# RWKV chunk products: which half of the partitions a chunk's rows stand on, from fp and bvp to zp

## The chip, the cores and the metric

The kernel runs on one core of a Trainium2 chip. The metric is the device time of one execution in microseconds (us), with everything loaded from and stored to the chip's memory; smaller is better. TensorE (PE) does the matmuls out of SBUF into PSUM, VectorE (DVE) and ScalarE (ACT) read PSUM, GpSimd (POOL) works on SBUF alone, and SyncE (SP) issues nearly all DMA transfers. Each engine works through its instructions strictly in the order of the built program and waits at an instruction whose inputs or whose buffer are not ready.

## The reference, cut to what matters

One decoder layer on a 2048 x 1024 input: an input projection feeds two mixers, stick-breaking attention (8 heads of 64) and RWKV-7 time mixing (8 heads of 64). Their outputs are gated, joined, projected and normalised. The part that matters here is the RWKV recurrence, which the kernel computes in chunks of 64 tokens:

```python
def step(state, inp):
    r_t, w_t, k_t, v_t, kk_t, b_t = inp
    sa = jnp.einsum('bhij,bhj->bhi', state, -kk_t)
    state = (state * w_t[:, :, None, :]
             + sa[..., None] * b_t[:, :, None, :]
             + v_t[..., None] * k_t[:, :, None, :])
    y_t = jnp.einsum('bhij,bhj->bhi', state, r_t)
    return state, y_t
_, y = lax.scan(step, state0, (tm(r), tm(decay), tm(k), tm(v), tm(kk), tm(kk * a)))
```

## The kernel before

The program has two parts. The attention part fills the first 1060 us of the profile and is not touched. The RWKV part follows: 16 blocks (4 pairs of heads x 4 stretches of 512 tokens), and from the 15th block on the output projection beside them, which then runs alone to the end.

A block holds 8 chunks of 64 tokens for 2 heads, so 16 independent pairs of chunk and head. Chunks are written c = 2i + e, with e the parity, and h is the head. Each step of a block is a **burst** of 16 small matmuls (fp32, contraction over 64 rows, 64 output rows), which the profile counts as 32 since it records each in two passes. A matmul of this size needs one quadrant of the 128 x 128 array: the half of the partitions on which its inputs stand gives the rows, the half on which its output stands gives the columns. `HS[0]` and `HS[1]` are the two halves.

The steps of one block, in the order of its own data, with the names under which the trace shows them (buffer numbers are left out, so `x1` is `x`, `t16` is `t`, `n2` is `n`, `y0` is `y`):

- `stage_p` projects three inputs k, r and v (`pss`, lines 356 to 358), each 24 matmuls of 128x512 in fp16. These 72 `pss` matmuls of a block are what PE does between the small steps. Lines 385 to 389 read a finished projection (a copy on ACT, then two copies and a multiply-add on DVE). `pn` (L910) and `n` (L924) normalise the keys; POOL makes `bk` and `ar` from them.
- `stage_x`: `x` (L960), two bursts, gives the chunk matrices `mn` and `mt` (DVE, L965). `mn` goes to memory and comes back as 16 x 16 blocks (L972, L974), DVE inverts these in small steps (`invert`, L775 to L802), and the inverses go to memory (`dt`, L978) and come back as the tile `t` (L983) on the halves that the matmuls want.
- `stage_t`: transposes, and `bvp` (L1019) into `ab`.
- `stage_l`: `fp` (L1033) from `t` and `mn`, masked by DVE into `ft` (L1037); then `xp` (L1042) and twice `xp` (L1052), each followed by DVE additions into `rf`.
- `stage_z`: `zp` (L1066) into two PSUM banks from `rf` and `ab`, copied by ACT into `at` (L1070) and `zg` (L1074); then `mr`, `np` and `y`.
- `stage_c`: the chain over the chunks, 8 `sp` matmuls with a DVE step after each, and `yr` (L1130).

In `bvp`, `fp` and `zp` the parity e alone decides the half: for `fp` and `zp` chunk e's inputs and outputs both stand on `HS[e]`, so the 16 matmuls use two of the four quadrants in turn, and `bvp` uses the other two. `x`, `mr` and `yr` already use all four: there parity and head give rows and columns.

Three blocks are worked on at once. While block n runs its chain, block n+1 is in stages t, l and z, and block n+2 in `stage_p` and `stage_x`. The stages are Python generators, merged by `_side`: each `yield` says how long the piece of work is taken to be, and the generator that is least far on goes next. This gives the order in which the program is written. A scheduler of the framework then orders each engine's instructions by it and by readiness; a `burst()` keeps its matmuls together and is pulled forward. PSUM has 8 banks here: ring `mm` of 3 (projections and other single results), ring `z` of 2 (`z_ps`), ring `tr` of 2, and one more. A new tile of a ring waits until the oldest bank's readers are done.

Of the kernel before, what the change touches and what calls it, by code (L numbers as in the profile page):

```python
# [12 lines left out]
AF = mybir.ActivationFunctionType  # L13
ALU = mybir.AluOpType
# [4 lines left out]
P = 128  # L19
# [6 lines left out]
def _bc(ap, shape):  # L26
    return ap.to_broadcast(shape)
# [61 lines left out]
def trunk(nc, a, out):  # L89
# [3 lines left out]
    PE, V, A, G, DMA = nc.tensor, nc.vector, nc.scalar, nc.gpsimd, nc.sync  # L93
# [27 lines left out]
    def z_ps(name="z"):  # L121
        return pp.tile([P, TB], F32, tag="z", bufs=NM[1], name=name)
# [821 lines left out]
    def stage_x(n):  # L944
# [5 lines left out]
        mn = B["mn"] = []  # L950
# [26 lines left out]
        for m in range(2):  # L977
            DMA.dma_start(out=bass.AP(tensor=dt.tensor, offset=dt.offset + m * 66560,  # L978
                                      ap=[[1040, 64], [64, 16], [1, 16]]), in_=view(pr, 256 * m, [16, 16], [1, 16]))
        t16 = B["t16"] = rw.tile([P, 2, 8, 64], F32, tag="t16", name="t16")  # L980
        for e in range(2):
            for m in range(2):
                DMA.dma_start(out=t16[HS[e], m], in_=dt[m, e].rearrange("c s t -> s c t")[0:64])  # L983

# [3 lines left out]
    def stage_t(n):  # L988
# [21 lines left out]
        for i in range(4):  # L1010
            PE.transpose(ap[:, i * P:(i + 1) * P], ar[:, 0, 2 * i:2 * i + 2].rearrange("p c t -> p (c t)"), ident)
        yield 0.44
        A.activation(out=ab[:, :, :, 0, :].rearrange("p i h d -> p (i h) d"),
                     in_=ap.rearrange("p (c d) -> p c d", c=8), func=AF.Copy)
        bvp = z_ps("bvp").rearrange("p (c d) -> p c d", c=8)
        with burst():
            for i, h in IH:
                for e in (1, 0):
                    PE.matmul(bvp[HS[e], 2 * i + h], mn[i // 2][HS[1 - e], e, i % 2, h], zg[HS[1 - e], e, i, h],  # L1019
                              start=True, stop=True)  # L1020
        yield 0.9
        A.activation(out=ab[:, :, :, 1, :].rearrange("p i h d -> p (i h) d"), in_=bvp, func=AF.Copy)

    def stage_l(n):
# [3 lines left out]
        rf = B["rf"] = rw.tile([P, 8, 64], F32, tag="rf", name="rf")  # L1028
        fp = z_ps("fp").rearrange("p (c d) -> p c d", c=8)
        with burst():  # L1030
            for i, h in IH:
                for e in (1, 0):
                    PE.matmul(fp[HS[e], 2 * i + h], mn[i // 2][HS[e], e, i % 2, h], t16[HS[e], 0, 2 * i + h],  # L1033
                              start=True, stop=True)
        yield 0.9
        ft = rw.tile([P, 8, 64], F32, tag="ft", name="ft")
        V.tensor_tensor(out=ft, in0=fp, in1=_bc(fmask, [P, 8, 64]), op=ALU.mult)  # L1037
        xp = z_ps("xp").rearrange("p (c d) -> p c d", c=8)
# [18 lines left out]
    def stage_z(n):  # L1057
# [3 lines left out]
        at = rw.tile([P, 4, 2, 64], F32, tag="at", name="at")  # L1061
        zp = [z_ps("zp").rearrange("p (c m d) -> p c m d", c=4, m=2) for _ in range(2)]
        with burst():
            for i, h in IH:
                for e in (1, 0):
                    PE.matmul(zp[i // 2][HS[e], 2 * (i % 2) + h].rearrange("p m d -> p (m d)"), rf[HS[e], 2 * i + h],  # L1066
                              ab[HS[e], i, h].rearrange("p m d -> p (m d)"), start=True, stop=True)
        yield 1.8
        for g in range(2):
            A.activation(out=at[:, 2 * g:2 * g + 2].rearrange("p i h d -> p (i h) d"), in_=zp[g][:, :, 0, :],  # L1070
                         func=AF.Copy)
        for g in range(2):
            for e in range(2):
                A.activation(out=zg[HS[e], e, 2 * g:2 * g + 2].rearrange("p i h d -> p (i h) d"),  # L1074
                             in_=zp[g][HS[e], :, 1, :], func=AF.Copy)
        rq = B["rq"] = rw.tile([P, 8, 64], F32, tag="rq", name="rq")
# [245 lines left out]
```

## Time and profile before

| what | value |
|---|---|
| median of 3 runs | 1924.12 us (1922.18 to 1925.9) |
| the profiled execution, time | 1919.86 us |
| the profiled execution, span from first to last instruction | 1918.1 us |
| mean granted clock of TensorE | 0.971 |
| PE busy over the span | 1699.1 us (89%) |
| DVE busy | 1380.4 us (72%) |
| ACT busy | 859.7 us (45%) |
| POOL busy | 774.4 us (40%) |
| RWKV part: 16 blocks, about 41 us each | 1062 to 1746 us |
| output projection alone | 1746 to 1918 us |

Busy shares count overlapping matmuls once, so a PE that is busy all the time may still have slow instructions in it. An engine's idle time matters only where another engine waits for it in turn. The time of an execution is its span plus 1.8 us.

### The profile page before, as it was taken

The page shows a single profiled execution, that of the slowest core. Times are in us where ns is not written, and L with a number is a line of the kernel's source. Part 1 is how long each engine was busy: PE and PEld are TensorE (multiplying, and loading weights), DVE is VectorE, ACT ScalarE, POOL GpSimd, SP SyncE. Part 2 cuts the span into 40 slices and gives each one's busy share as a digit, 9 for nine tenths or more (in the row PEclk, how much of TensorE's full clock was granted, in tenths as well). Part 3 has the DMA queues.
Part 4 walks back from the last instruction along what each step waited for, and adds up shares of the span by engine and source line. Part 5 has one row for each costly group of instructions (what it writes and reads, how often), then busy time and mean ns, then how long its engine had stood idle before and what let it go on. Part 6 is the DMA issues. An engine that isn't in the chain of part 4 may idle for free. (4 is left out here: it accounts for less than half of the span.)

```text
span 1918.1 us, 38809 instructions
## 1 busy us (share of the span) xinstructions
PE 1699.1 (89%) x14816; PEld 1164.2 (61%) x14816; DVE 1380.4 (72%) x2871; ACT 859.7 (45%) x1706; POOL 774.4 (40%) x1114
## 2 busy tenths in 40 slices
PE   1879978999899998999997888898899998989998
PEld 1546655666565665667654455665565655667886
DVE  8967697678785778768766557878777777765543
ACT  0556576456564666546644333333332333422221
POOL 3615465356553556445444123233233322223322
PEclk9989999999999999999989989999999999999999
DMA  8341201222122221132111523322332333335442
GB/s 296 112 144 45 70 25 45 64 75 64 42 56 75 61 67 41 51 79 69 54 45 39 154 49 86 69 62 77 77 80 77 86 78 104 80 92 169 149 138 88
DMA packets 210408, 159.93 MB, mean 83 GB/s; under 512 B 113247, under 2 KB 171820, under 8 KB 210222
## 3 DMA queue, kind: packets, MB, share of 16 engines
q1 hardware_dynamic: 209220, 155.31, 28.8%
q8 instruction: 117, 1.92, 0.4%
q10 hardware_dynamic: 1002, 2.13, 0.4%
q14 instruction: 69, 0.57, 0.1%
HBM read 94.48 MB, written 44.04 MB: 72 GB/s over the span
## 5 line engine op out<-in xcount | busy, mean ns | idle before, releaser
L509 POOL TENSOR_TENSOR s<-s,u 128x512 f32<-128x512 f32 (+2 forms) x320 | 306.0, 964 | 219.6 <-ACT s L497 99.7
L526 DVE TENSOR_TENSOR al<-tr,ah 128x512 fp32r<-128x512 f32 (+1 forms) x320 | 187.3, 598 | 98.0 <-ACT ah L525 97.2
L508 DVE TENSOR_TENSOR_SCAN u<-u,dmask 128x512 f32<-128x512 f32 x192 | 239.8, 1267 | 13.7 <-ACT u L496 12.1
L525 ACT ACTIVATE ah<-tr 128x512 fp32r<-128x512 f32 (+1 forms) x320 | 171.9, 553 | 104.8 <-PE tr L521 101.5
L496 ACT ACTIVATE u<-z 128x512 f32<-128x512 f32 (+2 forms) x320 | 173.4, 556 | 73.4 <-PE z L493 48.1
L521 PE MATMUL tr<-kept_ident,s 128*128 128x128 f32 x1088 | 174.2, 280 | 32.8 <-DVE al L526 26.2
L497 ACT ACTIVATE s<-z 128x512 f32<-128x512 f32 (+2 forms) x320 | 166.2, 549 | 54.6 <-PE tr L521 54.6
L521 PEld LDWEIGHTS tr<-kept_ident,s 128*128 128x128 f32 x1088 | 130.9, 143 | 74.5 <-DVE al L526 37.5
L356 PE MATMUL pss<-kept_hh,kept_wh 128*128 128x512 f16 x416 | 160.4, 386 | 8.8 <-PEq L716 8.8
L357 PE MATMUL pss<-kept_hl,kept_wh 128*128 128x512 f16 x416 | 160.3, 385 | 0.0
L358 PE MATMUL pss<-kept_hh,kept_wl 128*128 128x512 f16 x416 | 160.3, 385 | 0.0
L358 PEld LDWEIGHTS <-kept_wl 128*128 128x128 f16 x928 | 93.3, 101 | 105.1 <-issue 14.2
L356 PEld LDWEIGHTS <-kept_wh 128*128 128x128 f16 x928 | 94.5, 102 | 101.5 <-issue 29.8
L357 PEld LDWEIGHTS <-kept_wh 128*128 128x128 f16 x928 | 93.3, 100 | 92.8 <-issue 23.1
L492 PE MATMUL z<-kt,qt 128*128 128x512 f32 (+2 forms) x320 | 132.2, 418 | 10.4 <-ACT s L497 4.4
L539 PE MATMUL av<-ah,vt 128*128 128x512 f32 (+1 forms) x320 | 136.6, 427 | 4.8 <-DVE o L550 2.3
L540 PE MATMUL av<-al,vt 128*128 128x512 f32 (+1 forms) x320 | 136.3, 427 | 0.2 <-DVE al L526 0.2
L493 PE MATMUL z<-kt,qt 128*128 128x512 f32 (+2 forms) x320 | 117.5, 371 | 0.0
L505 DVE TENSOR_TENSOR_SCAN u<-u,dmask 128x128 f32<-128x128 f32 (+3 forms) x128 | 107.2, 866 | 12.2 <-ACT u L496 6.6
L356 PE MATMUL psg<-kept_hh,kept_wh 128*128 128x512 f16 x256 | 100.4, 392 | 8.2 <-DVE klo L420 3.1
L1260 PE MATMUL po<-kept_woh,kept_yh 128*128 128x512 f32 x256 | 103.3, 404 | 0.0
L1261 PE MATMUL po<-kept_wol,kept_yh 128*128 128x512 f32 x256 | 101.9, 398 | 0.0
(292 smaller groups left out, 4167.0 us busy)
## 6 DMA issues: line engine op xcount, KB each, us to landing
kept_raw<-in_w_in SPq DMA_DIRECT2D x29, 512.0 KB, 3.9
ad<-in_ada_w SPq DMA_DIRECT2D x24, 512.0 KB, 5.4
qt<-qt SPq DMA_DIRECT2D x48, 256.0 KB, 3.4
xt<-in_x SPq DMA_DIRECT2D x16, 512.0 KB, 5.2
y<-sg SPq DMA_DIRECT2D x32, 256.0 KB, 2.0
t<-dt SPq DMA_DIRECT2D x64, 128.0 KB, 3.1
xr<-in_x SPq DMA_DIRECT2D x16, 512.0 KB, 3.6
out<-xr SPq DMA_DIRECT2D x16, 512.0 KB, 2.6
```

The costliest lines, as they stand in the source:

```text
L356: PE.matmul(ps, wh[:, k], hth[b][:, k], start=k == 0, stop=False)
L357: PE.matmul(ps, wh[:, k], htl[b][:, k], start=False, stop=False)
L358: PE.matmul(ps, wl[:, k], hth[b][:, k], start=False, stop=k == KB - 1)
L496: A.activation(out=u[:, 0:nk], in_=z[:, 0:nk], func=AF.Sigmoid, scale=-0.125)
L497: A.activation(out=s[:, 0:nk], in_=z[:, 0:nk], func=AF.Sigmoid, scale=0.125)
L508: V.tensor_tensor_scan(out=ur, data0=ur, data1=mr, initial=u[:, nk:nk + 1], op0=ALU.mult, op1=ALU.bypass)
L509: G.tensor_tensor(out=s[:, 0:nk], in0=s[:, 0:nk], in1=u[:, 1:nk + 1], op=ALU.mult)
L521: PE.transpose(tp[:, q * P:(q + 1) * P], att[gi, q][:, ks * P:(ks + 1) * P], ident)
L525: A.activation(out=ah[:, r], in_=tp[:, r], func=AF.Copy)
L526: V.tensor_tensor(out=al[:, r], in0=tp[:, r], in1=ah[:, r].bitcast(F32), op=ALU.subtract)
L539: PE.matmul(av[:, r], vs, ah[:, r], start=first, stop=False, skip_group_check=True)
L540: ins = PE.matmul(av[:, r], vs, al[:, r], start=False, stop=last, skip_group_check=True)
```

## The change

From `fp` and `bvp` on to `zp` a chunk's rows stand on the half given by parity plus head, `e ^ h`, and no longer on `HS[e]`. So:

- `bvp` and `fp` each write two PSUM banks, one from ring `z` and one from ring `mm`, half a bank filled in each; a bank belongs to one half of rows. `zp` has two banks as before, now by `e ^ h` and no longer by chunk number, so both banks are written from the first matmuls to the last.
- The readers follow: `ft` is made in two DVE pieces of 128x256 and no longer in one of 128x512; `ab` in four ACT pieces of 64x256 from `ap` (one of 128x512 before) and two of 128x256 from `bvp` (one before); `at` in four ACT pieces of 64x256 (two of 128x256 before). `zg` stays at four pieces.
- The second half of the tile `t` (m = 1) has to be loaded to the new halves: two loads of half the size in place of one, for each parity. A block loads `t` with 6 DMAs, 4 before.
- The yields after `fp`, `bvp` and `zp` are halved (0.9 to 0.5, 1.8 to 0.9), so the order in which the program is written changes too.

```diff
 t16 = B["t16"] = rw.tile([P, 2, 8, 64], F32, tag="t16", name="t16")
 for e in range(2):
-    for m in range(2):
-        DMA.dma_start(out=t16[HS[e], m], in_=dt[m, e].rearrange("c s t -> s c t")[0:64])
+    DMA.dma_start(out=t16[HS[e], 0], in_=dt[0, e].rearrange("c s t -> s c t")[0:64])
+    for f in range(2):
+        DMA.dma_start(out=t16[HS[f], 1].rearrange("p (i x) t -> p i x t", x=2)[:, :, e],
+                      in_=dt[1, e].rearrange("(i h) s t -> h s i t", h=2)[e ^ f, 0:64])
...
-A.activation(out=ab[:, :, :, 0, :].rearrange("p i h d -> p (i h) d"),
-             in_=ap.rearrange("p (c d) -> p c d", c=8), func=AF.Copy)
-bvp = z_ps("bvp").rearrange("p (c d) -> p c d", c=8)
+apv = ap.rearrange("p (i h d) -> p i h d", i=4, h=2)
+for h in range(2):
+    for e in range(2):
+        A.activation(out=ab[HS[e ^ h], :, e, 0, :], in_=apv[HS[e], :, h, :], func=AF.Copy)
+bvp = [f("bvp").rearrange("p (i d) -> p i d", i=8) for f in (z_ps, mm_ps)]
...
-            PE.matmul(bvp[HS[e], 2 * i + h], mn[i // 2][HS[1 - e], e, i % 2, h], zg[HS[1 - e], e, i, h],
+            PE.matmul(bvp[e][HS[e ^ h], i], mn[i // 2][HS[1 - e], e, i % 2, h], zg[HS[1 - e], e, i, h],
...
-yield 0.9
-A.activation(out=ab[:, :, :, 1, :].rearrange("p i h d -> p (i h) d"), in_=bvp, func=AF.Copy)
+yield 0.5
+for e in range(2):
+    A.activation(out=ab[:, :, e, 1, :], in_=bvp[e][:, 0:4], func=AF.Copy)
...
-fp = z_ps("fp").rearrange("p (c d) -> p c d", c=8)
+fp = [f("fp").rearrange("p (i d) -> p i d", i=8) for f in (z_ps, mm_ps)]
...
-            PE.matmul(fp[HS[e], 2 * i + h], mn[i // 2][HS[e], e, i % 2, h], t16[HS[e], 0, 2 * i + h],
+            PE.matmul(fp[e][HS[e ^ h], i], mn[i // 2][HS[e], e, i % 2, h], t16[HS[e], 0, 2 * i + h],
...
-yield 0.9
+yield 0.5
...
-V.tensor_tensor(out=ft, in0=fp, in1=_bc(fmask, [P, 8, 64]), op=ALU.mult)
+for e in range(2):
+    V.tensor_tensor(out=ft[:, e::2], in0=fp[e][:, 0:4], in1=_bc(fmask, [P, 4, 64]), op=ALU.mult)
...
-            PE.matmul(zp[i // 2][HS[e], 2 * (i % 2) + h].rearrange("p m d -> p (m d)"), rf[HS[e], 2 * i + h],
-                      ab[HS[e], i, h].rearrange("p m d -> p (m d)"), start=True, stop=True)
-yield 1.8
-for g in range(2):
-    A.activation(out=at[:, 2 * g:2 * g + 2].rearrange("p i h d -> p (i h) d"), in_=zp[g][:, :, 0, :],
-                 func=AF.Copy)
+            f = e ^ h
+            PE.matmul(zp[f][HS[e], i].rearrange("p m d -> p (m d)"), rf[HS[f], 2 * i + e],
+                      ab[HS[f], i, e].rearrange("p m d -> p (m d)"), start=True, stop=True)
+yield 0.9
+for e in range(2):
+    for h in range(2):
+        A.activation(out=at[HS[e], :, h, :], in_=zp[e ^ h][HS[e], :, 0, :], func=AF.Copy)
```

The order of the built program moves in three places.

First, TensorE in an ordinary block, around `fp` (the seventh block; `pss` with `wh_263` is projection k before, `wh_237` is projection r after). Before:

```order
L356 MATMUL pss<-kept_hh_987,kept_wh_263 128x512
L1033 MATMUL fp<-t_21457,mn 64x64 x16
L357 LDWEIGHTS kept_wh_263
L357 MATMUL pss<-kept_hl_988,kept_wh_263 128x512
L358 LDWEIGHTS kept_wl_264
L358 MATMUL pss<-kept_hh_987,kept_wl_264 128x512
```

Now:

```order
L358 MATMUL pss<-kept_hh_987,kept_wl_238 128x512
L1041 MATMUL fp<-t_21563,mn 64x64 x16
L910 MATMUL pn<-kept_hm_214,sq 128x2 x4
L1051 MATMUL xp<-t_21563,ft 64x64 x16
L924 MATMUL n_21894<-kept_ident_61,nr 128x128 x4
L356 LDWEIGHTS kept_wh_263
L356 MATMUL pss<-kept_hh_987,kept_wh_263 128x512
```

Before, four `pss` stand between `fp` and `xp`, and `pn` and `n` stand 21 and 11 `pss` ahead of `fp`. Now `fp` stands right behind the 24th and last matmul of projection r, `pn` is all that stands between `fp` and `xp`, and `n` follows `xp`. Further on, where the order before has `x`, `zp`, one `pss`, `x`, the order now has `x`, one matmul of `zp`, four `pss`, the other fifteen of `zp`, nine `pss`, `x`.

Second, TensorE in the third block, where `fp` moves far ahead (`ytp` is a transpose of the block before). Now:

```order
L358 MATMUL pss<-kept_hh_987,kept_wl_264 128x512
L1169 MATMUL ytp<-kept_ident_61,ysb 128x128 x4
L356 LDWEIGHTS kept_wh_263
L356 MATMUL pss<-kept_hh_987,kept_wh_263 128x512
L357 LDWEIGHTS kept_wh_263
L357 MATMUL pss<-kept_hl_988,kept_wh_263 128x512
L358 LDWEIGHTS kept_wl_264
L358 MATMUL pss<-kept_hh_987,kept_wl_264 128x512
L1041 MATMUL fp<-t_19364,mn 64x64 x16
```

Before, 15 `pss`, `pn`, 6 `pss`, `n` and 7 `pss` stand between `ytp` and `fp` of this block; now 3 `pss`. Counted from the block's own last burst of `x` to its `fp`, 52 `pss` have become 26 in the third block and 69 have become 38 in the second. In the first block, 35 `pss`, `pn`, `n` and 4 `pss` between `bvp` and `fp` have become 11 `pss`. From the fourth block on the count falls by about 5, with `pn` and `n` gone from that stretch too.

Third, ScalarE after `zp` (`y` is the copy that follows). Before:

```order
L1070 ACTIVATE at<-zp 128x256
L1074 ACTIVATE zg<-zp 64x256 x2
L1070 ACTIVATE at<-zp 128x256
L1074 ACTIVATE zg<-zp 64x256 x2
L385 ACTIVATE t_22053<-pss,kept_um_19937 128x512
```

Now:

```order
L915 ACTIVATE nr<-nt 128x512
L1081 ACTIVATE at<-zp 64x4x64 x4
L1084 ACTIVATE zg<-zp 64x4x64 x4
L1113 ACTIVATE y_22683<-y_22600 128x512
```

Before, three pieces empty the first bank of `zp` while the second is still being written. Now all eight pieces come after the whole burst, and each bank's last reader is among the last two; the second burst of `x` takes over the bank whose last reader is the seventh.

## Rows read from the trace of the kernel before

**Rows 1.** Busy time by stretch; columns: stretch, length, engines, PEclk, DMA.

```profile
1103.60:1110.50 6.90, 5.57 (x46) 4.04 (x48) 1.49 (x4) 0.67 (x2) 5.46 (x6) 0.56 0.01 2
1210.00:1249.60 39.60, 35.98 (x520) 23.94 (x518) 32.70 (x102) 13.84 (x25) 12.30 (x12) 1.00 0.36 80
```

**Rows 2.** Waits of PE in the RWKV blocks: total us, times, longest.

```profile
PE zp L1066 <- DVE mt L965: 13.0, 11, 1.5
PE pn L910 <- ACT sq L902: 9.7, 9, 3.8
...
PE n L924 <- ACT nr L915: 3.3, 5, 1.2
```

**Rows 3.** Timeline of PE in one block; columns: start, length, what, [idle before].

```profile
1235.14 1.15 PE L1033 MATMUL fp<-t,mn 64*64 64x64 f32 x32
1236.22 0.39 PE L358 MATMUL pss<-kept_hh,kept_wl 128*128 128x512 f16 x1
...
1237.18 1.15 PE L1042 MATMUL xp<-t,ft 64*64 64x64 f32 x32
...
1241.67 0.69 PE L1130 MATMUL yr<-sall,rq 64*64 64x64 f32 x32
...
1243.07 1.04 PE L1066 MATMUL zp<-ab,rf 64*64 64x128 f32 x16
1245.34 1.09 PE L1066 MATMUL zp<-ab,rf 64*64 64x128 f32 x16 [1.23 <-DVE mt L965]
...
1246.68 1.10 PE L960 MATMUL x<-ar,bk 64*64 64x128 f32 x32
```

**Rows 4.** The same block earlier, timeline of PE: pn and n.

```profile
1230.62 1.05 PE L910 MATMUL pn<-kept_hm,sq 128*128 128x2 f32 x8 [0.20 <-ACT sq L902]
1231.53 0.38 PE L356 MATMUL pss<-kept_hh,kept_wh 128*128 128x512 f16 x1
...
1233.47 0.65 PE L924 MATMUL n<-kept_ident,nr 128*128 128x128 f32 x4
1233.96 0.38 PE L356 MATMUL pss<-kept_hh,kept_wh 128*128 128x512 f16 x1
```

**Rows 5.** The same block, timeline of DVE: rt (reader of projection r) and ft.

```profile
1235.60 0.74 DVE L389 SCALAR_TENSOR_TENSOR rt<-pss,kept_u,t 128x512 f32<-128x512 f32 x1
1236.33 0.69 DVE L1037 TENSOR_TENSOR ft<-fp,kept_fmask 128x512 f32<-128x512 f32 x1
```

**Rows 6.** First block, timeline of ACT: zp is emptied.

```profile
1118.43 0.38 ACT L1070 ACTIVATE at<-zp 128x256 f32<-128x256 f32 x1 [4.36 <-PE zp L1066]
1118.71 0.76 ACT L1074 ACTIVATE zg<-zp 64x256 f32<-64x256 f32 x2
```

**Rows 7.** First and last of 12 blocks, timeline of PE: x, and that block's fp.

```profile
1207.17 1.10 PE L960 MATMUL x<-ar,bk 64*64 64x128 f32 x32
...
1656.49 1.10 PE L960 MATMUL x<-ar,bk 64*64 64x128 f32 x32
...
1685.80 1.15 PE L1033 MATMUL fp<-t,mn 64*64 64x64 f32 x32
```

**Rows 8.** The same two blocks, timeline of SP: the loads of t.

```profile
1226.83 2.65 SPq L983 DMA_DIRECT2D t<-dt  x4
...
1679.20 2.64 SPq L983 DMA_DIRECT2D t<-dt  x4
```

**Rows 9.** Tile t in blocks 2 to 15, and in the first block: issue to landing.

```profile
DMA to landing us min/median/max: 2.7/3.1/4.5
...
L983 SPq DMA_DIRECT2D t<-dt x4: 574/610/627, 1098.6 to 1100.7; - x4
DMA to landing us min/median/max: 2.8/2.8/2.8
```

**Rows 10.** First block, timeline of PE: the pss ahead of pn, and pn.

```profile
1099.51 0.38 PE L358 MATMUL pss<-kept_hh,kept_wl 128*128 128x512 f16 x1
1103.69 1.87 PE L910 MATMUL pn<-kept_hm,sq 128*128 128x2 f32 x8 [3.80 <-ACT sq L902]
```

More of the change, by code (lines that the diff above doesn't have):

```diff
@@ L1061, in stage_z @@
         at = rw.tile([P, 4, 2, 64], F32, tag="at", name="at")
-        zp = [z_ps("zp").rearrange("p (c m d) -> p c m d", c=4, m=2) for _ in range(2)]
+        zp = [z_ps("zp").rearrange("p (i m d) -> p i m d", i=4, m=2) for _ in range(2)]
         with burst():
@@ L1065, in stage_z @@
                 for e in (1, 0):
-                    PE.matmul(zp[i // 2][HS[e], 2 * (i % 2) + h].rearrange("p m d -> p (m d)"), rf[HS[e], 2 * i + h],
-                              ab[HS[e], i, h].rearrange("p m d -> p (m d)"), start=True, stop=True)
-        yield 1.8
-        for g in range(2):
-            A.activation(out=at[:, 2 * g:2 * g + 2].rearrange("p i h d -> p (i h) d"), in_=zp[g][:, :, 0, :],
-                         func=AF.Copy)
[L1072 to L1075, printed above, removed]
+                    f = e ^ h
[5 more added lines that the diff above has]
+                A.activation(out=at[HS[e], :, h, :], in_=zp[e ^ h][HS[e], :, 0, :], func=AF.Copy)
+        for e in range(2):
+            for h in range(2):
+                A.activation(out=zg[HS[e], e, :, h, :], in_=zp[e ^ h][HS[e], :, 1, :], func=AF.Copy)
         rq = B["rq"] = rw.tile([P, 8, 64], F32, tag="rq", name="rq")
```

## The prediction

> **What bounds the kernel now.** I read the busy time by stretch first. In an ordinary RWKV block PE works 36.0 of 39.6 us at the full granted clock, DVE 32.7, ACT 13.8 [rows 1]. So PE is the bound here, and time can leave a block in two ways: fewer microseconds of PE work, or fewer of the 3.6 us in which PE waits. The list of PE's waits says what those are: the second half of `zp` waits for DVE's `mt` (13.0 us in 11 blocks), `pn` for ACT (9.7 us, 3.8 of them once, in the first block), `n` for ACT (3.3) [rows 2, 10]. None of them is for `t`: before `fp` something else has always taken longer.
>
> Next the timeline of PE in one block. A burst of 64x64 on two quadrants (`fp`) lasts 1.15 us, one on four (`yr`) 0.69. `zp`, 64x128 on two quadrants, takes 1.04 + 1.09; `x`, 64x128 on four, takes 1.10 with twice the records [rows 3]. Between `fp` and `xp` lie 2.04 us, with four `pss` in them [rows 3]. A `pss` costs 0.215 from start to start: nine of them lie between 1231.53 and 1233.47. In the same way `pn` costs 0.9 and `n` 0.5 [rows 4].
>
> Last the way of `t`, which nobody waits for today: it decides what the moved `fp` will find. Between the second burst of `x` and the first load of `t` there are 18.6 us in the first of the 12 blocks from the fourth to the fifteenth and 21.6 in the last [rows 7, 8]; the mean of all twelve is 20.0. To `fp` there are 26.9 and 28.2 [rows 3, 7], mean 27.9. Four loads take 2.65 us on SP, some 0.66 each, and a load lands 3.1 us after its issue (2.7 to 4.5) [rows 8, 9].
>
> **The bursts.** `bvp` and `fp` fall from 1.15 to 0.69: -0.46 each. `zp` falls from 2.13 to 1.10: -1.0. That is 1.46 a block for the two; `fp`, before and behind which PE now waits for others, is counted below. These durations are the surest numbers of the sum: the same shapes already run on four quadrants in `x` and `yr`.
>
> **pn and n.** They move behind `fp`. By then ACT has long finished for them, and their waits go: 13.0 us in all less 5.0 in the first block, over 13 blocks, is -0.6 a block [rows 2].
>
> **fp to xp.** Before, 2.04 less four `pss` is 1.18 of its own. Now `fp` stands directly behind the last `pss` of projection r. DVE's `rt`, which reads r, ended 1.2 us after `fp` began [rows 5], with two `pss` between; now that is about 1.7 after the place of `fp`. The two pieces of `ft` stand behind it on DVE, at 0.4 each (estimate: the one piece of double size took 0.69 [rows 5]). So `xp` starts 2.6 after, with 0.9 of `pn` in between: 1.7 of its own, +0.5. Bounds: +0.2, if `rt` comes earlier; +0.8, if each piece costs the whole 0.69.
>
> **The wait for t.** `fp` reads the halves m = 0, which the fourth of the six loads completes in most blocks. From `x` that makes 20.0 + 2.05 + 3.1 = 25.2 us. PE's own way there was 27.9; from it go `pn` and `n` (1.4), five `pss` (1.1), `bvp` (0.46) and the waits of `pn` and `n` (0.6): 24.4. `fp` is thus late by 0.8 on average, with a scatter of about 1 (the margin between load and `fp` was 8.3 in the first of the twelve and 6.6 in the last). The first microsecond costs nothing more, since PE would only wait for `rt` afterwards instead; what exceeds it comes to +0.4, by the scatter. Bounds: 0 if the loads go out 1 us sooner, +1.6 if all are as late after `x` as in the last block (21.6).
>
> **The second burst of x.** It takes over the bank whose last reader is the seventh of ACT's eight pieces. A piece costs 0.38 alone, 0.28 where it overlaps the next [rows 6]: seven end 2.0 to 2.7 after `zp`, plus some 0.1 of start. PE has nine `pss`, 1.94, to do meanwhile. The wait is 0.1 to 0.9; I take +0.5. The four pieces of `ab` and two of `bvp` lie on an ACT that is idle two thirds of the block [rows 1], and `bvp`'s results are wanted only at `zp`, 15 us later: nothing.
>
> **The sum of an ordinary block.** -0.46 - 1.0 - 0.6 + 0.5 + 0.4 + 0.5 = -0.66; over twelve blocks -8. The wait of `zp` for `mt` stays, since `x` is still split around it.
>
> **The first three blocks.** Here `fp` moves ahead by far more than `t` has room for. In the first, the 35th `pss` behind `bvp` started at 1099.5 [rows 10]; `fp` now stands behind the 11th, 24 x 0.215 = 5.2 earlier, at 1094.1 to the end of that matmul with the shorter `bvp`. The loads begin at 1098.6, the fourth issues at 1100.7 and lands 2.8 later, at 1103.5 [rows 9], and with six loads no sooner. PE stands still for 9.4 us. In the second block 31 `pss` go from the stretch and in the third 26, so `fp` is reached 6.7 and 5.6 earlier than it was, plus 2.5 for `pn`, `n`, waits and `bvp`: 27.9 becomes 18.7 and 19.8 against 25.2, or 6.5 and 5.4 of waiting. Together 21 us. Against them stand the waits of the first block's `pn` and `n` (-5.0), the bursts (3 x 1.46 = -4.4), and the 81 displaced `pss`, 17 us of work that comes later in places where PE waited: of that I take a third, -6 (bounds 0 and -12). After the first block's waits of today the granted clock is 0.56 over 6.9 us [rows 1], and `pn` takes 1.87 instead of 1.05 [rows 4, 10]: that is the lower level of 1.2 GHz. Two more such falls cost some +1. Net +7. The last block, which has no `pss`, gains 1.
>
> Behind this stands a rule: by the Trainium skill, "TensorE: Matmul & The Clock Gate", "What's actually happening", an array left idle falls to 1.2 GHz and must first be busy again to return to 2.4. The row agrees, and the rule adds nothing to the sum.
>
> **Total**: -8 + 7 - 1, with the roundings -3, so 1917 where the profiled execution took 1919.9 (span 1918.1). Against the median of the three runs, 1924.1, that is 1921. A measurement of this kernel tells about 0.2%, 3.9 us, from no change; this forecast lies just inside.
>
> **The rivals.**
>
> B, the gain comes through. If SP issues `t` sooner, as the inverse on DVE may come sooner when `ft` and the rest are early, then 0.9 of waiting (0.4 + 0.5) a block falls away, -11, and the first three blocks lose half as much, -6: 1904. For it: the loads follow work on DVE that has its own time and that a shorter block could pull ahead. Against it: 20.0 us of the 25.2 are a chain of DVE steps and transfers that the change does not touch.
>
> C, slower: the chain of `t` becomes the bound. Each further microsecond by which `t` lands later than forecast costs 12, since every block from the fourth on then waits at `fp` with nothing to cover it. From +0.25 us a block on, the kernel is slower than before. At 21.6 after `x`, which the last of the twelve blocks shows, it is +1.6 x 12 = +19: 1940. For it: two more loads on SP, and 3.6 us of slack in a block of which most goes. Against it: `t` had 1.5 to 3.2 us to spare in these two blocks (6.6 and 8.3 from load to `fp`, less 5.15), and PE lets go of 3.6, so the lateness begins near nothing.
>
> C2, ACT becomes the gate of `zp`. Eight pieces at 0.38 are 3.04 us, and none can begin before the burst is over. If they don't overlap, the seventh ends 2.8 after `zp`; with `nr` or a copy of `pss` in front of them the second `x` waits 1.1 instead of 0.5: +7, 1928. For it: three pieces used to be done while the second half was being written. Against it: ACT sat idle for 4.36 us before `zp` [rows 6].
> The Trainium skill, "TensorEngine Tiling (Array Packing)", "PSUM Bottleneck", speaks against the change in this sense: packing speeds up TensorE, not the emptying of PSUM, which may then be the bottleneck.
>
> D, the bursts stay as long as they are (the quadrants don't overlap when the matmuls come from two banks in this order): +1.46 x 16 = +23: 1944. Against it: `x` and `yr`.
>
> **Chances.** Forecast 0.50, its own range 1909 to 1927: 0.22 faster by over 0.2%, 0.20 within, 0.08 slower. B 0.22, faster. C 0.18, slower. C2 0.07: 0.02 within, 0.05 slower. D 0.03, slower. Faster 0.44, same 0.22, slower 0.34. The range 1902 to 1940 reaches from B to C and leaves D and the ends of B and C out.
>
> **What would show it.** Bursts of `bvp` and `fp` of 0.7 us and a `zp` of 1.1 in the timeline; if not, D. In the list of PE's waits a new `fp`, for the transfer of `t`: some 20 us from three waits, and about 1 us in most later blocks; if it is 2 or more in each, C; if near none, B. A second `x` that waits for ACT's `zg` 0.5 a block; if 1 or more, C2. No more waits at `pn` and `n`. A granted clock that falls in the first three blocks. The forecast is wrong above all if the 20.0 us between `x` and the loads change.

## The result: 2.5% slower, and the profile after

The changed kernel took 1969.8 us (median of 4 runs, 1967.8 to 1971.7) where the kernel before took 1923.2 in the same session: a ratio of 1.0247, 95% interval 1.0229 to 1.0265. Forecast were 1921 and a range of 1902 to 1940. The profiled execution has a span of 1970.0 us, 51.9 more than the one before; the medians lie 46.6 apart.

Where the time went can be read from one event of every block, the start of `fp`. These are starts in the traces; the rows are [rows 3, 7] for the kernel before and stand in the timeline below for the changed one.

| | before | changed | difference | forecast |
|---|---|---|---|---|
| `fp` of the fourth block | 1235.1 | 1265.2 | +30.1 | +7 |
| `fp` of the fifteenth block | 1685.8 | 1733.8 | +48.0 | 0 |
| mean period of these 11 blocks | 40.97 | 42.59 | +1.62 | -0.66 |
| end of the span | 1918.1 | 1970.0 | +51.9 | -3 |

So two things went wrong, one in the first three blocks and one in each ordinary block, with signs or sizes that the sum did not have. The last 3.9 us fall behind the fifteenth `fp`.

A start counted from the beginning of the profile also holds the attention part, which no edit touches and which does not end at the same time in every execution. The first `pss` of the RWKV part, behind PE's wait between the two parts, shows it; the rows are from the kernel before, from the changed one and from e12, a run below:

```profile
1054.57 0.58 PE L356 MATMUL pss<-kept_hh,kept_wh 128*128 128x512 f16 x1 [8.79 <-PEq L716]
1055.60 0.59 PE L356 MATMUL pss<-kept_hh,kept_wh 128*128 128x512 f16 x1 [8.78 <-PEq L716]
1063.56 0.59 PE L356 MATMUL pss<-kept_hh,kept_wh 128*128 128x512 f16 x1 [8.78 <-PEq L717]
```

Over all sixteen traces it starts between 1054.5 and 1064.3. Counted from there, the fourth `fp` stands at 180.6 before and at 209.6 now, which is +29.0 for the first blocks.

First the list of PE's waits from 1062 to 1800 us (total, times, longest), which answers to [rows 2]:

```profile
PE fp L1041 <- DMA t<-dt: 47.5, 11, 10.0
PE sp L1129 <- DVE sall L1130: 11.1, 12, 2.1
PE x L960 <- POOL ar L932: 9.3, 3, 4.0
PE zp L1076 <- DVE mt L965: 8.3, 9, 0.9
...
PE x L960 <- ACT zg L1084: 3.5, 9, 0.4
```

`pn` is gone from the list and `n` nearly so, as forecast. `fp` is new at its head, 47.5 us. A second new one was not forecast: the first burst of `x` waits for POOL's `ar`. Third, the second `x` waits for ACT, only 0.4 at a time.

The timeline of PE shows both places, first the four early `fp` with the `x` that follow them, then the last ordinary block's `fp`:

```profile
1105.32 1.23 PE L1041 MATMUL fp<-t,mn 64*64 64x64 f32 x32 [9.97 <-DMA t<-dt]
1107.88 1.98 PE L1051 MATMUL xp<-t,ft 64*64 64x64 f32 x32
...
1127.21 3.64 PE L960 MATMUL x<-ar,bk 64*64 64x128 f32 x64 [2.24 <-POOL ar L932]
...
1156.36 1.23 PE L1041 MATMUL fp<-t,mn 64*64 64x64 f32 x32 [7.37 <-DMA t<-dt]
...
1175.27 1.98 PE L960 MATMUL x<-ar,bk 64*64 64x128 f32 x32 [3.12 <-POOL ar L932]
...
1210.86 1.23 PE L1041 MATMUL fp<-t,mn 64*64 64x64 f32 x32 [7.61 <-DMA t<-dt]
1229.83 1.99 PE L960 MATMUL x<-ar,bk 64*64 64x128 f32 x32 [3.98 <-POOL ar L932]
...
1265.21 0.81 PE L1041 MATMUL fp<-t,mn 64*64 64x64 f32 x32 [3.32 <-DMA t<-dt]
...
1733.75 0.81 PE L1041 MATMUL fp<-t,mn 64*64 64x64 f32 x32 [4.02 <-DMA t<-dt]
```

The reader should see a chain and not a list: PE stands 10.0 us at `fp`, and the projection r that `ar` needs is queued behind it on PE, so that the next `x` is late as well and waits a second time; a late `x` makes a late `t`, and the next `fp` waits again. DVE's `rt`, which reads r, ends at 1125.90, POOL makes `ar` from it until 1127.16, and the `x` at 1127.21 starts with it. The waits of these four `fp` and three `x` add up to 28.3 + 9.3 = 37.6 us.

An ordinary block around `zp`, same view, which answers to [rows 3]:

```profile
1439.42 1.05 PE L960 MATMUL x<-ar,bk 64*64 64x128 f32 x32
1440.31 0.38 PE L1076 MATMUL zp<-ab,rf 64*64 64x128 f32 x2
...
1442.57 1.10 PE L1076 MATMUL zp<-ab,rf 64*64 64x128 f32 x30 [0.92 <-DVE mt L965]
1443.60 0.39 PE L358 MATMUL pss<-kept_hh,kept_wl 128*128 128x512 f16 x1
...
1445.34 0.38 PE L357 MATMUL pss<-kept_hl,kept_wh 128*128 128x512 f16 x1
1446.11 1.11 PE L960 MATMUL x<-ar,bk 64*64 64x128 f32 x32 [0.39 <-ACT zg L1084]
1447.04 1.05 PE L1091 MATMUL mr<-mt,at 64*64 64x128 f32 x32
```

and ACT in the same stretch, which answers to [rows 6]:

```profile
1443.70 1.31 ACT L1081 ACTIVATE at<-zp 64x256 f32<-64x256 f32 x4 [11.13 <-PE zp L1076]
1445.02 1.31 ACT L1084 ACTIVATE zg<-zp 64x256 f32<-64x256 f32 x4
```

`zp` is as short as forecast, 1.10. But the second `x` starts 6.69 us after the first (1439.42 to 1446.11), where it was 4.50 before (1242.18 to 1246.68, [rows 3]). Nine `pss` fill most of that time, so PE hardly waits; what is late is `x` itself, and with it half of `mn`, the blocks that go to memory, and `t`. Nine of the twelve blocks from the fourth to the fifteenth are like this one; in the other three the two bursts lie 1.8 us apart, before and now. The mean distance of the twelve (the **gap** in what follows) has grown from 3.82 to 5.51, by 1.7, and the period by 1.6.

### The profile page after: what moved, and what is told of

The parts are those of the page before. It is cut to its first block, busy times and chain, and to the rows that moved or that the text cites. A ratio compares the mean times of both kernels' runs of the same rounds, so it can differ in the third digit from the quotient of the medians.

```text
span 1970.0 us, 38917 instructions
## 1 busy us (share of the span) xinstructions
PE 1700.8 (86%) x14816; PEld 1159.2 (59%) x14816; DVE 1377.4 (70%) x2887; ACT 883.0 (45%) x1802; POOL 777.3 (39%) x1114
## 5 line engine op out<-in xcount | busy, mean ns | idle before, releaser
L508 DVE TENSOR_TENSOR_SCAN u<-u,dmask 128x512 f32<-128x512 f32 x192 | 240.0, 1268 | 12.9 <-ACT u L496 11.4
L521 PEld LDWEIGHTS tr<-kept_ident,s 128*128 128x128 f32 x1088 | 130.7, 144 | 74.1 <-DVE al L526 37.6
L916 POOL TENSOR_TENSOR ar<-kn,ep 128x512 f32<-128x512 f32 x15 | 28.5, 1900 | 199.3 <-ACT kn L900 199.3
L333 POOL TENSOR_TENSOR kept_raw<-kept_raw,rkw 128x1024 f32<-128x1024 f32 x29 | 56.7, 1956 | 126.0 <-DVE rkw L332 99.0
```

The costliest lines, as they stand in the source:

```text
L508: V.tensor_tensor_scan(out=ur, data0=ur, data1=mr, initial=u[:, nk:nk + 1], op0=ALU.mult, op1=ALU.bypass)
L521: PE.transpose(tp[:, q * P:(q + 1) * P], att[gi, q][:, ks * P:(ks + 1) * P], ident)
```

## The experiments

All times are medians; the interval is that of the ratio to the kernel before, run on the same chip. The last three columns are from one trace of each kernel: "`fp` 4" is the start of `fp` in the fourth block, counted from the first `pss` of the RWKV part; "gap" is the mean time from the first to the second burst of `x` over the fourth to the fifteenth block; "period" is the mean from `fp` to `fp` over the same blocks. No kernel was traced twice, so small differences in these columns are not told from chance.

| run | median us | ratio, 95% interval | `fp` 4 | gap | period |
|---|---|---|---|---|---|
| before | 1923.2 to 1925.8 | 1 | 180.6 | 3.82 | 40.97 |
| changed | 1969.8 | 1.0247 (1.0229 to 1.0265) | 209.6 | 5.51 | 42.59 |
| e1, `fp` in ring tr | 1956.5 | 1.0159 (1.0135 to 1.0183) | 192.3 | 5.67 | 42.84 |
| e2, before with `fp` in ring mm | 1929.8 | 1.0025 (1.0008 to 1.0041) | 190.3 | 3.81 | 40.65 |
| e3, old yields | 1960.2 | 1.0194 (1.0159 to 1.0228) | 190.7 | 5.46 | 42.46 |
| e4, before with new yields | 1934.0 | 1.0043 (1.0022 to 1.0064) | 194.4 | 3.89 | 40.46 |
| e5, `zp` in ring tr | 1945.4 | 1.0120 (1.0098 to 1.0142) | 204.4 | 2.77 | 40.54 |
| e6, `zp` and `fp` in ring tr | 1934.2 | 1.0063 (1.0040 to 1.0087) | 198.4 | 3.00 | 40.28 |
| e7, before with `zp`'s banks filled in turn | 1941.3 | 1.0093 (1.0064 to 1.0122) | 185.8 | 4.73 | 41.70 |
| e8, loads for `fp` written first | 1973.9 | 1.0266 (1.0241 to 1.0291) | 208.8 | 5.52 | 42.55 |
| e9, e6 with old yields | 1921.6 | 0.9997 (0.9984 to 1.0010) | 185.6 | 2.65 | 40.21 |
| e10, e9 with `zp` in tr and z | 1919.1 | 0.9976 (0.9958 to 0.9994) | 183.5 | 3.32 | 39.95 |
| e11, `zp` by bank | 1965.7 | 1.0227 (1.0201 to 1.0254) | 208.4 | 4.10 | 41.79 |
| e12, before, 6 `pss` fewer a block | 1924.0 | 0.9990 (0.9971 to 1.0009) | 186.7 | 3.68 | 40.71 |
| e13, before, more DVE work | 1927.4 | 1.0016 (0.9991 to 1.0041) | 183.0 | 3.81 | 41.17 |
| e14, before, 6 `pss` more a block | 1935.8 | 1.0055 (1.0035 to 1.0074) | 178.2 | 3.67 | 41.91 |

**First round: where `fp`'s bank stands.** The first theory (RING) was that `fp`'s second bank, which comes from the projections' ring mm, ties `fp` to its turn in that ring. The rivals were the loads (LOADS) and the yields (YIELDS).

e1 gives `fp`'s second bank to another ring:

```diff
-fp = [f("fp").rearrange("p (i d) -> p i d", i=8) for f in (z_ps, mm_ps)]
+fp = [f("fp").rearrange("p (i d) -> p i d", i=8) for f in (z_ps, tr_ps)]
```

> The changed kernel with one edit: the second bank of fp comes from ring tr (mr and yr use it) and no longer from ring mm (projections, pn, n). Layout, six loads of t, all ACT pieces and the halved yields stay. Theory RING (fp's bank in ring mm ties fp to its turn among the projections, so it is written ahead of pn and n, PE stands at fp, and the way of t from x to fp becomes the period of the blocks): the order of before comes back and the shorter bursts remain, 1900, between 1890 and 1912. Rival LOADS (two more loads and ACT's eight pieces make t and the second x late): still 1955 to 1970. Rival YIELDS (the halved yields pull stages t, l, z ahead): still 1955 to 1970.

1956.5: far from RING's number, within the range of its rivals. In the built order `fp` stands behind `pn` and `n` again, and its waits for `t` are gone; the early blocks give back 17 us. But the period stays at 42.84. The list of PE's waits of e1 has a new head, and the timeline of one block shows where it is:

```profile
PE x L960 <- ACT zg L1084: 22.2, 10, 2.5
...
1602.06 1.05 PE L960 MATMUL x<-ar,bk 64*64 64x128 f32 x32
...
1605.21 1.10 PE L1076 MATMUL zp<-ab,rf 64*64 64x128 f32 x30 [0.92 <-DVE mt L965]
1608.75 1.10 PE L960 MATMUL x<-ar,bk 64*64 64x128 f32 x32 [2.11 <-ACT zg L1084]
```

Here no nine `pss` lie in front of the second `x`, and it is as late as in the changed kernel, 6.69 us after the first. The same delay was hidden from the list of waits in one kernel and shows in it in the other.

e2 does the ring part alone, in the kernel before:

```diff
-fp = z_ps("fp").rearrange("p (c d) -> p c d", c=8)
+fp = mm_ps("fp").rearrange("p (c d) -> p c d", c=8)
```

> The kernel before with one edit: its only fp bank comes from ring mm in place of ring z. No other layout, four loads, old yields, two quadrants. RING: slower than before by 20 to 50 us, 1943 to 1973, with PE waiting for t at fp. LOADS and YIELDS: as before, 1918 to 1930.

1929.8. The mechanism is there (PE's wait of `fp` for `t` is 21.6 us in 4 times, the longest 9.3) and the early blocks cost 10 us, but the ordinary ones don't slow down, they are a little quicker. RING explains a part of the early blocks and nothing else; as a cause of the whole it fell.

e3 gives the changed kernel the yields of before after `bvp`, `fp` and `zp`, and e4 does the reverse in the kernel before:

```diff
-yield 0.5
+yield 0.9
...
-yield 0.5
+yield 0.9
...
-yield 0.9
+yield 1.8
```

> The changed kernel with the three yields of before (0.9, 0.9, 1.8). The first two blocks keep their early fp, from the third on fp stands 21 to 24 pss behind ytp. RING: the wait of the third block shrinks by about 10 us, the rest stays: 1955, between 1945 and 1966. YIELDS: 1900 to 1925. LOADS: 1965 to 1975.

> The kernel before with the halved yields (0.5, 0.5, 0.9) and nothing else. RING and LOADS: 1915 to 1932, no wait of more than 5 us in all at fp. YIELDS: 1945 or more.

1960.2 and 1934.0: the halved yields cost about 10 us either way, and more than all of it before the fourth `fp` (-19 in e3, +14 in e4; in e4 the ordinary blocks give 6 of that back). YIELDS as the main cause fell, but the 1934 also lie just over what RING and LOADS allowed: a part of the loss is theirs.

**Second round: when `zp`'s banks come free.** The new theory (EVICT) took up what e1's timeline showed. e5 takes both banks of `zp` from a ring that `x` does not use:

```diff
-zp = [z_ps("zp").rearrange("p (i m d) -> p i m d", i=4, m=2) for _ in range(2)]
+zp = [tr_ps("zp").rearrange("p (i m d) -> p i m d", i=4, m=2) for _ in range(2)]
```

> The changed kernel with one edit: zp's two banks come from ring tr and no longer from ring z. fp stays in ring mm, yields, loads and ACT pieces stay. Theory EVICT (both banks of zp fill to the end, ACT then reads them in eight pieces, and the second burst of x, which needs a bank of ring z, waits for the seventh; so every block's second x, and with it its t, is some 2 us later, and in the ordinary blocks the period grows by 2): the ordinary blocks lose those 2 us again, the first blocks stay slow by fp's bank: 1943, between 1932 and 1952; x's two bursts end 5 to 6 us after the first begins, not 7.8. Rival LOADS (six loads of t in place of four): 1962 to 1972.

1945.4, as EVICT had it, from a one-word edit that leaves every instruction's shape alone. The timeline of PE in e5 shows the second `x` 1.8 us behind the first, so that the two bursts end 2.9 after the first begins and not 5 to 6, as expected. It also shows who waits now:

```profile
1389.18 1.10 PE L960 MATMUL x<-ar,bk 64*64 64x128 f32 x32 [0.88 <-POOL ar L932]
1390.11 1.05 PE L1076 MATMUL zp<-ab,rf 64*64 64x128 f32 x32
1390.98 1.05 PE L960 MATMUL x<-ar,bk 64*64 64x128 f32 x32
1393.63 1.37 PE L1091 MATMUL mr<-mt,at 64*64 64x128 f32 x32 [1.59 <-ACT zg L1084]
```

`mr`, whose banks are now the late ones, waits 1.6 for the same ACT pieces. That wait is visible and cheap (e10 below takes most of it away and gains 2.5 us); the earlier one was hidden and dear, since `x` and not `mr` starts the way of `t`. The gap falls by 2.74 and the period by 2.05, to 40.54.

e6 is e5 and e1 together:

> The changed kernel with zp's two banks and fp's second bank from ring tr. EVICT: the first blocks go as before and the ordinary ones too, less the shorter bursts: 1912, between 1895 and 1925. LOADS: 1945 to 1957, as with fp's bank alone.

1934.2, between the two forecasts: the gains add (24 us for `zp`, 11 more for `fp`) and LOADS misses by more, but 11 us over the kernel before remain, with `fp` 4 at 198.4, near the 194.4 that the yields alone gave in e4.

e7 delays `zp`'s first bank in the kernel before, with two quadrants, four loads and the six old ACT pieces:

```diff
-for i, h in IH:
+for i, h in [(i, h) for i in (0, 2, 1, 3) for h in range(2)]:
     for e in (1, 0):
         PE.matmul(zp[i // 2][HS[e], 2 * (i % 2) + h].rearrange("p m d -> p (m d)"), rf[HS[e], 2 * i + h],
...
```

> The kernel before with one edit: zp's matmuls go through the pairs of chunks in the order 0, 2, 1, 3, so that its two banks are filled in turn and the first one is full only near the end. Two quadrants, four loads, old yields, two large and four small ACT pieces stay. EVICT: ACT can start on the first bank only after three quarters of zp, the second x comes 0.5 to 1.5 us later in each block: 1938, between 1930 and 1950. LOADS: 1918 to 1930.

1941.3. The order of sixteen matmuls inside one burst costs 18 us. Its timeline has the second `x` 5.64 us behind the first, with a wait for ACT in front. Part of the 1.14 added there is `zp` itself, since three quarters of it and no longer half now stand behind the wait for DVE's `mt` (1.53 us in place of 1.09 [rows 3]):

```profile
1256.31 1.06 PE L960 MATMUL x<-ar,bk 64*64 64x128 f32 x32
1257.20 0.60 PE L1066 MATMUL zp<-ab,rf 64*64 64x128 f32 x8
1259.46 1.53 PE L1066 MATMUL zp<-ab,rf 64*64 64x128 f32 x24 [1.34 <-DVE mt L965]
1261.95 1.10 PE L960 MATMUL x<-ar,bk 64*64 64x128 f32 x32 [0.96 <-ACT zg L1074]
```

e8 writes the loads that `fp` reads ahead of the others:

```diff
 for e in range(2):
     DMA.dma_start(out=t16[HS[e], 0], in_=dt[0, e].rearrange("c s t -> s c t")[0:64])
+for e in range(2):
     for f in range(2):
         DMA.dma_start(out=t16[HS[f], 1].rearrange("p (i x) t -> p i x t", x=2)[:, :, e],
```

> The changed kernel with the two loads that fp reads (m = 0) written first and the four others behind them. Nothing else. fp can then start 1.3 us earlier after the first load. EVICT: fp comes earlier in the blocks in which it waits for t, xp then waits for the other loads; 1960, between 1952 and 1970. LOADS: the time of the six loads is the whole loss: 1935 to 1950.

1973.9, no gain, and outside EVICT's range too. But the edit hardly tested anything. The timeline of SP in the second block of e8 (L983 are the two loads that `fp` reads, L986 the four others) shows two of the others issued first:

```profile
1153.41 1.25 SPq L986 DMA_DIRECT2D t<-dt  x2
1154.71 1.28 SPq L983 DMA_DIRECT2D t<-dt  x2
1156.04 1.29 SPq L986 DMA_DIRECT2D t<-dt  x2
```

That is the built order of the changed kernel as well. Only four of the sixteen blocks of e8 issue the two loads first; in the first block `fp` starts 3.7 us after the first load in place of 5.2. PE's wait of `fp` for `t` is 43.2 us in place of 47.5. So e8 decides nothing about LOADS. What speaks against it is e5, far outside its range, and e9 below, which has all six loads and the time of the kernel before.

**Third round: what remains.** e9 is e6 with the yields of before, and e10 is e9 with one bank of `zp` from each ring, the tr bank emptied first. The cut shows what e10 does to `zp`, against the changed kernel:

```diff
-zp = [z_ps("zp").rearrange("p (i m d) -> p i m d", i=4, m=2) for _ in range(2)]
+zp = [f("zp").rearrange("p (i m d) -> p i m d", i=4, m=2) for f in (tr_ps, z_ps)]
...
-for e in range(2):
-    for h in range(2):
-        A.activation(out=zg[HS[e], e, :, h, :], in_=zp[e ^ h][HS[e], :, 1, :], func=AF.Copy)
+for f in range(2):
+    for e in range(2):
+        A.activation(out=zg[HS[e], e, :, e ^ f, :], in_=zp[f][HS[e], :, 1, :], func=AF.Copy)
```

> The changed kernel with zp's two banks and fp's second bank from ring tr, and with the three yields of before. Theory THREE CAUSES (zp's banks, fp's bank and the yields make up the loss, some 24, 11 and 10 us): 1924, between 1915 and 1932, equal to before, since mr now waits for zp's banks where the second x waited. Rival REST (something in the layout itself, the loads or the many ACT pieces, costs 10 us): 1930 to 1938.

> As the kernel with zp and fp in ring tr and old yields, but zp has one bank of ring tr and one of ring z, and ACT empties the tr bank first. Then neither the second x nor the first half of mr waits for a bank of zp that is still being read. THREE CAUSES: the wait of mr (1.7 us a block) goes and the shorter bursts are left over: 1908, between 1895 and 1918. REST: 1922 to 1932.

e9 took 1921.6, equal to before: three causes make up the whole loss (24 for `zp`'s banks, 11 for `fp`'s, 13 for the yields, undone in this order; alone, `fp`'s bank gave 13 in e1 and the yields 10 in e3). e10 took 1919.1, 0.24% faster than before, interval 0.06% to 0.42%; it is the best version, but far from the 1908 expected. The lists of PE's waits, e9 first, show what the removed wait turned into:

```profile
PE mr L1091 <- ACT zg L1084: 23.9, 16, 2.4
PE pn L910 <- ACT sq L902: 17.4, 14, 4.4
```

```profile
PE sp L1129 <- DVE sall L1130: 17.7, 24, 2.2
PE pn L910 <- ACT sq L902: 16.7, 15, 4.3
PE x L960 <- DVE mt L965: 7.7, 9, 1.1
PE mr L1091 <- ACT zg L1084: 6.4, 8, 1.3
```

`mr` waits 17.5 us less, and 2.5 us of that reach the time. In both, `pn` waits 7 to 8 us longer than in [rows 2]: PE gets there sooner, ACT does not.

e11 keeps the changed kernel and orders `zp` by bank, so that it runs on two quadrants again and its first bank is full at half time:

```diff
-for i, h in IH:
-    for e in (1, 0):
-        f = e ^ h
+for f, i, e in [(f, i, e) for f in range(2) for i in range(4) for e in (1, 0)]:
+        h = e ^ f
...
+for f in range(2):
+    for e in range(2):
+        h = e ^ f
+        A.activation(out=at[HS[e], :, h, :], in_=zp[f][HS[e], :, 0, :], func=AF.Copy)
+        A.activation(out=zg[HS[e], e, :, h, :], in_=zp[f][HS[e], :, 1, :], func=AF.Copy)
```

> The changed kernel with zp's matmuls ordered by bank, so that zp runs on two quadrants at a time again and its first bank is full at half time; ACT reads that bank's four pieces first. fp's bank and yields stay as changed. THREE CAUSES: what counts of zp is when its first bank is emptied, so the slower burst is the faster kernel: 1950, between 1940 and 1960. REST, or four quadrants as such a gain: 1970 or more.

1965.7, a miss: the period falls by 0.8 where 2 were expected, 4 us in all. The gap falls with it, by 1.4, to 4.10. So the three kernels that differ in `zp` alone stand in one order: gap 5.51, 4.10 and 2.77, period 42.59, 41.79 and 40.54 (changed, e11, e5). Emptying early helps less than a ring of its own, here beside waits of `x` for `ar` of 11.4 us in six places between 1190 and 1700, where the changed kernel has one of 4.0. How much of the rest is the longer burst was not separated.

**Fourth round: what a microsecond of PE is worth.** The forecast's first step was that PE is the bound. e12 takes PE work from the kernel before (two of the eight third products in each of the three projections are left out, which makes them less exact), e14 adds as much, and e13 adds DVE work instead:

```diff
-            PE.matmul(ps, wl[:, k], hth[b][:, k], start=False, stop=k == KB - 1)
+            if not (lean and k in (2, 5)):
+                PE.matmul(ps, wl[:, k], hth[b][:, k], start=False, stop=k == KB - 1)
```

```diff
+            if more and k in (2, 5):
+                PE.matmul(ps, wl[:, k], htl[b][:, k], start=False, stop=False)
             PE.matmul(ps, wl[:, k], hth[b][:, k], start=False, stop=k == KB - 1)
```

```diff
-V.scalar_tensor_tensor(out=dst, in0=ps, scalar=u1, in1=t2[:, 0:TB], op0=ALU.mult, op1=ALU.add)
+for _ in range(2 if mrow in ("k", "v") else 1):
+    V.scalar_tensor_tensor(out=dst, in0=ps, scalar=u1, in1=t2[:, 0:TB], op0=ALU.mult, op1=ALU.add)
```

> The kernel before without the third matmul (rounded part of the weight by the inputs) at two of the eight row blocks in each of the projections k, r and v: six pss of 72 fewer in a block, 1.29 us of PE work, and less exact projections. It measures what a microsecond of PE's work is worth in this kernel. PE BOUND (the first step of the prediction: the time falls by what PE no longer does): 16 x 1.29 = 21 us less, 1902, between 1897 and 1908. CHAIN (PE waits for DVE and ACT between the steps of a block, and work taken from it turns partly into waits): 5 to 14 us less, 1909 to 1918.

> The kernel before with a fourth product (rounded part of the weight by rounded part of the input) at two of the eight row blocks in each of the projections k, r and v: six pss more in a block, 1.29 us of PE work. PE BOUND: 21 us more, 1945, between 1938 and 1952. DVE CHAIN: 0 to 8 us more, 1925 to 1933. The order is made anew with them, which alone may cost or give some us.

> The kernel before with DVE's last step of the projections k and v done twice (the same inputs, the same output): 1.48 us more of DVE work in each block, some of it on the way to pn. DVE CHAIN (the steps that pass through DVE set the period of the blocks, so its time counts in full): 16 x 1.48 = 24 us more, 1948, between 1938 and 1955. PE BOUND: within 6 us of before. Between them: both count in part.

21 us of PE work taken away change the time by -1.8, interval -5.6 to +1.7: nothing that can be measured, and outside the ranges of both theories. 21 us more cost 10.3, between the two ranges. And 24 us of DVE work more cost 1.9, interval -1.7 to +7.9, far below the 1938 that DVE CHAIN had as its least. (The lines view of e13 has them: 32 `kt` and 32 `vt` steps of 0.74 each, 16 of each before.)

```profile
L390 DVE SCALAR_TENSOR_TENSOR vt<-pss,kept_u,t 128x512 f32<-128x512 f32 x32 | 23.7, 742 | 0.1
L390 DVE SCALAR_TENSOR_TENSOR kt<-pss,kept_u,t 128x512 f32<-128x512 f32 x32 | 23.7, 739 | 0.0
```

So neither engine's work alone sets the period, but PE's is not free either: in the traces 1.29 us less a block shorten the period by 0.26, and 1.29 us more lengthen it by 0.94. e12 and e14 also change the built order, and e12's trace loses 6 us before the fourth `fp`, so they give the size and not an exact rate.

## Why the prediction was wrong, step by step

**Right: the bursts, but for `fp`.** `bvp` takes 0.69 and `zp` 1.10, as priced. `fp` takes 0.7 in the three blocks in which nothing is waited for in front of it; in the other thirteen, each behind a wait, it takes 0.81 to 1.25. **Right: pn and n.** Their waits are gone (0.5 us is left at `n`). Right as a size, too, was the second `x`'s wait for ACT: 0.4 in the nine blocks that have it, against 0.5.

**Failed first: "The second burst of x".** The step asked how long PE waits in front of that burst, found 0.5, and stopped there. It did not ask what begins with it. The burst is the head of the chain `x`, `mn`, memory, inverse, memory, `t`, `fp`, and the next block's `x` comes behind that `fp`, so the chain closes on itself. The burst became 2.2 us later in nine blocks of twelve, and the `t` wait's step took its 20.0 us from the end of that same burst, in which the delay cannot be seen: in the changed kernel they are 20.5. The sign that the prediction named above all others, a change of these 20.0, was watched at the wrong end. e5 and e7 show the cause from both sides: with the banks freed the period falls by 2.05 us, more than the 1.62 that it had lost, and a late first bank alone costs the kernel before 0.73 us a block, for a gap that is 0.91 longer. Of the rivals C2 had the place (ACT as the gate behind `zp`) at +7, and C the way of working (`t`'s chain as the bound); the runs show them as one thing: ACT's gate feeds C's chain, at 24 us.

The Trainium skill says in "TensorEngine Tiling (Array Packing)", "PSUM Bottleneck", that packing speeds up TensorE but not the emptying of PSUM, which may become the bottleneck. These runs agree, with a turn: ACT was idle 11.13 us before `zp`, so its throughput was no limit. What counted was that no bank is full before the burst ends, and that the next tile in line for that bank was one with a long chain behind it (e5, e7).

**Failed second: "The first three blocks".** The idle time was foreseen, 21 us in three waits at `fp`; 25.0 were measured, and 3.3 in a fourth. What failed were the credits of 15 against it: the displaced `pss` do not fill later holes. They are what POOL's `ar` needs, so PE makes `x` late by standing still, waits 9.3 us more for it, and the loop hands the delay on. +7 became +29. e1 to e4 show the causes: the bank in ring mm (17 us of it go when that alone is undone, 10 come when it alone is done) and the yields (19 go, 14 come). The two overlap, since together they would be more than the whole.

**Failed third: the first sentence, that PE is the bound.** From 36.0 of 39.6 us busy [rows 1] the sum took every microsecond of PE work at full price. e12 shows that 1.29 us less a block move the time by nothing measurable, e14 that the like amount more costs half its length. In e10, with the three causes undone, 1.0 of the 1.46 us a block is kept in the period but 4 us of 23 in the time; in its trace the first blocks and the stretch behind the fifteenth `fp` are longer than before, by 3.0 and 3.5.

**Put at nothing: the clock in the ordinary blocks.** The sum priced a lower clock in the first blocks only, at +1. Over the eleven periods from the fourth `fp` to the fifteenth the granted clock is 0.99 before and 0.95 now (rows at the end), and PE is busy 403.5 us in place of 407.2: 3.7 less, where the shorter bursts alone are 16. In e9, at 0.99, it is 391.7, 15.6 less. One place where it falls is behind `fp`, where only `pn` is left to do until `ft` is ready; in six of the twelve blocks from the fourth to the fifteenth the `xp` that follows takes 1.97 or 1.98, before in none of them. How much of the period's 1.62 goes this way was not separated; e7 has the late second `x` at a clock of 0.99.

**The wait for t** was forecast as 0.4 beyond what `rt` hides. Its size from the first load on was right: where `fp` waits 2 us or more for `t`, it starts 4.9 to 5.3 us after that load, and 5.15 were priced. The wait was nothing in five of the twelve ordinary blocks and 1 to 4 us in the others, 1.8 on the mean; that this is the loop's delay, which arrives there, is argued and not shown. The prediction's first step also read the list wrongly: one wait of PE in the list behind [rows 2] is for `t`, in the last block, which has no `pss`:

```profile
PE fp L1033 <- DMA t<-dt: 3.6, 1, 3.6
```

**What stays open:** what sets the 41 us of an ordinary block of the kernel before. Not PE's work and not DVE's alone; a chain of waits through several engines is the likeliest, but no run isolated it.

## What to carry to other kernels

When an edit lets a burst fill two buffers side by side and no longer one after the other, ask which tile takes over the buffer that used to come free early, and what starts with that tile; the wait in front of it may be covered by filler work and still be the dearest in the program. Before pricing an engine's saved time at full value because it is 90% busy, take the same amount of work from it in one run: here that run (e12) says nothing measurable. When runs are compared by a start in the trace, count it from the first instruction behind the part that the edit leaves alone. And a tile that an edit moves into another ring also moves in the order of that ring's users: a producer that waits for memory does not belong in the ring of the work that should fill the wait.

## What was not expected of the hardware

A piece that ACT reads from PSUM costs by its columns and not by its partitions: in the kernel before, `zg` from `zp` (64x256) takes 0.37 us on the mean and `at` (128x256) 0.38, `zg` from `vp` (64x512) 0.59 and `ab` from `ap` (128x512) 0.60. Cutting a copy in two along the partitions thus nearly doubles it, and the eight pieces take 2.62 us where two large and four small ones were partly done during the burst.

After its 10 us of idle PE is slow for some microseconds, which the prediction foresaw. The stretches show it (columns as in [rows 1]): in the first PE stands still for `t`, the second is what follows.

```profile
1095.00:1105.30 10.30, 0.35 (x2) 0.00 (x0) 4.66 (x11) 2.44 (x4) 2.71 (x4) 0.74 0.41 88
1105.30:1113.00 7.70, 7.68 (x114) 5.25 (x115) 2.28 (x6) 0.00 (x0) 2.40 (x3) 0.68 0.02 5
```

The granted clock is 0.68 in the second, a mean over the two levels of 1.2 and 2.4 GHz, and the `xp` burst in it takes 1.98 us where it takes 1.15 at the higher one [rows 3]. The Trainium skill, "TensorE: Matmul & The Clock Gate", "What's actually happening", says the same of an array that was left idle.

What it did not foresee is the same thing in ordinary blocks, behind much shorter waits. Here is the `xp` of the block shown above, with a `pss` that follows it, then the stretch in which both lie, and then the eleven periods, before and now:

```profile
1431.57 1.97 PE L1051 MATMUL xp<-t,ft 64*64 64x64 f32 x32 [1.59 <-DVE ft L1046]
...
1434.38 0.63 PE L356 MATMUL pss<-kept_hh,kept_wh 128*128 128x512 f16 x1
```

```profile
1431.60:1435.00 3.40, 3.40 (x38) 2.75 (x38) 1.27 (x3) 0.63 (x1) 1.79 (x2) 0.50 0.36 114
```

```profile
1235.10:1685.80 450.70, 407.22 (x5631) 267.86 (x5630) 343.63 (x1035) 152.27 (x275) 134.84 (x119) 0.99 0.32 81
1265.20:1733.80 468.60, 403.48 (x5617) 261.64 (x5618) 340.45 (x1046) 167.82 (x339) 134.83 (x118) 0.95 0.31 78
```

The granted clock is 0.50 in the short stretch, the lower level, and 1.00 in the 4 us before `fp`. The `xp` takes 1.97 and the `pss` 0.63, where an `xp` takes 1.15 and a `pss` 0.38 in [rows 3, 4].
